# Two streaming encoder layers on one core: sums of squares moved to TensorE, additions to VectorE, eight early products in the first layer

## The chip, the cores and the metric

The kernel runs on one core of one Trainium2 chip. The metric is the device time of one execution in microseconds (us); smaller is better. The five engines of the core run their own queues in order and wait for each other through semaphores. In the profile they are PE (TensorE, with its weight loads as PEld), DVE (VectorE), ACT (ScalarE), POOL (GpSimd) and SP (SyncE, which issues the loads).

## What is computed

A hybrid encoder of two layers works on 256 frames of a new stream and 64 frames of a running one, so 320 token columns with 1024 features. Each layer is a mixer and a ConvFFN, each between two RMS norms. The first layer's mixer is a Mamba-2 scan, the second one's is latent attention (MLA). After the first layer the shared key latent is made from the stream. Cut to what the change touches:

```python
def rmsnorm(x, g):
    y = xf * lax.rsqrt(jnp.mean(xf * xf, axis=-1, keepdims=True) + EPS)
    return y * g
for layer in range(2):
    h = rmsnorm(x, norm_mix_pre[layer])
    mix = mamba2_mixer(h, ...) if layer == 0 else mla_attend(h, ...)
    x = x + rmsnorm(mix, norm_mix_post[layer])
    f = conv_ffn(rmsnorm(x, norm_ffn_pre[layer]), ...)
    x = x + rmsnorm(f, norm_ffn_post[layer])
```

## The kernel before

Features lie on the 128 partitions and tokens on the free axis, so x is eight tiles of 128x320 (k = 0 to 7). Every fp32 product is made of three matmuls of split operands, a high and a low part each (`xgh` and `xgl`, `wh` and `wl`): high by high, low by high, high by low. ACT makes the high parts, DVE the low parts. All weights stream in by SP's loads into `wr` and are split into `wh` and `wl` before use.

**A join** is the place where one part ends and the next begins: `x = x + y * r`, where `y` holds the part's output and `r` the factor of its post norm. There are three joins, and `enter` (boundary=True) writes them: into ffn 0 (at 269 us), into MLA (at 512 us) and into ffn 1 (at 735 us). `late_rstd` sums the squares of the last output on PE, makes the factor on POOL (`newton`), and `spread` broadcasts it over the partitions by three PE transposes into a PSUM tile (`pr` or `px`). Then, for each k, DVE multiplies `y` by the spread tile, adds it to x (POOL does this for k = 3, 5, 7), ACT makes `xgh` and DVE `xgl` one step behind, and ACT squares the new x (`xsq`). POOL adds the squares into `xacc`. The order on DVE and ACT in a join is as written; the other engines' orders come from a scheduler.

The next part's matmuls start with raw x: `outer` runs k over the outside, so that six output blocks (three and three in MLA) take 18 matmuls for each k as soon as `xgh` and `xgl` of that k exist. The factor of the pre norm comes later: `rstd_of` sums `xacc` over the partitions on PE (`toksum`, three 128x1 matmuls), `mean` and `newton` make the factor, and it is spread into `xr` and multiplied onto the block's results. Blocks that come still later use normalized x instead: `normalized` makes `xn` = x times `xr` on POOL and splits it into `xnh` and `xnl`.

**The first layer's start** is `enter` with boundary=False: x is loaded, split and squared, and blocks 0 to 3 are done with k outside. Blocks 3 to 7 of the next loop follow with raw x. The convolutions (`conv`) of the first six blocks are done by a small POOL copy of padding rows into `ext`, two DVE products of the PSUM block with `xr` into `ext` (these free the PSUM buffer), a POOL copy of the saved rows to `ssave`, one ACT and three DVE operations. The eight `xn` steps are put between those blocks, with two `xn` buffers.

Of the kernel before, what the change touches and what calls it, by code (L numbers as in the profile page):

```python
# [11 lines left out]
AF = mybir.ActivationFunctionType  # L12
# [29 lines left out]
RING = 2, 3, 2  # L42
EARLY = 1, 9, 3
HIGH = 2, 0, 2
# [42 lines left out]
class Kern:  # L87
# [254 lines left out]

    def mean(self, src, dim, pool):

        v = self.t(pool, [P, 3], "nwv", bufs=3)
        self.nc.vector.tensor_scalar(v, src, 1.0 / dim, EPS, op0=ALU.mult, op1=ALU.add)
        return v
# [7 lines left out]
    def spread(self, r, ps=None):  # L355

        ps = self.pr() if ps is None else ps
        for c, l0 in enumerate(TOK):
            self.pe_end = self.nc.tensor.transpose(ps[:, l0:l0 + 128], r[:, c:c + 1].to_broadcast([P, P]), self.ident).ins
        return ps[:, :T]  # L360
# [37 lines left out]

    def enter(self, xgp, sp, tag, g=None, boundary=True):

# [5 lines left out]
        xl = self.t(xgp, [P, KD, T], "xgl", F32R, bufs=1)  # L406
        acc = self.t(sp, [P, T], "xacc", bufs=1)
        self.xhigh = []
# [19 lines left out]
        def square(k):  # L428
            if k == 0:
                act(out=acc, in_=self.x[:, k, :], func=AF.Square)  # L430
                return
            s = self.t(sp, [P, T], tag, bufs=2)
            act(out=s, in_=self.x[:, k, :], func=AF.Square)
            nc.gpsimd.tensor_tensor(out=acc, in0=acc, in1=s, op=ALU.add)  # L434

        with self.region if boundary else ExitStack():
            for k in range(KD + 1):
                if k < KD:
                    xk = self.x[:, k, :]
                    if boundary:  # L440
                        yk = self.y[:, k, :]
                        tt(out=yk, in0=yk, in1=r, op=ALU.mult)
                        if k == 0:
                            tt(out=xh[:, k, :], in0=xk, in1=yk, op=ALU.add)
                        e = nc.gpsimd if k in (3, 5, 7) else nc.vector
                        e.tensor_tensor(out=xk, in0=xk, in1=yk, op=ALU.add)
                        if k:
                            high(k)
                        else:
                            low(k)  # L450
                    else:
                        high(k)
                        low(k)
                if boundary and k > 1:
                    low(k - 1)
                if k:
                    square(k - 1)
        if boundary:
            self.ends.pop(0)
        return xh, xl, acc  # L460

    def normalized(self, xgp, sp, g, rstd):

        nc = self.nc
        xh = self.t(xgp, [P, KD, T], "xnh", F32R, bufs=1)
        xl = self.t(xgp, [P, KD, T], "xnl", F32R, bufs=1)

        def step(k):
            xn = self.t(sp, [P, T], "xn", bufs=2)
            nc.gpsimd.tensor_tensor(out=xn, in0=self.x[:, k, :], in1=rstd, op=ALU.mult)  # L470
            self.split(xh[:, k, :], xl[:, k, :], xn, self.v(g, k))

        return xh, xl, [lambda k=k: step(k) for k in range(KD)]
# [115 lines left out]

    def outer(self, nblk, xh, xl, xacc, pool):  # L590
# [51 lines left out]

    def conv(self, ps, rstd, pool, k, pads, w, b, rows_out, dst=None):

# [3 lines left out]
        q = m + TP  # L648
        both = pads.shape[1] == 2 * m
        ext = self.t(pool, [P, 2 * q if both else W], "ext", bufs=3)  # L650
        if both:
            nc.gpsimd.tensor_copy(out=ext.rearrange("p (a b) -> p a b", a=2)[:, :, 0:m], in_=pads.rearrange("p (a b) -> p a b", a=2))
# [8 lines left out]
        if both:  # L661
            nc.gpsimd.tensor_copy(out=rows_out, in_=ext[:, TP:TP + 2 * (TS + m)].rearrange("p (a b) -> p a b", a=2)[:, :, 0:m])
        else:
# [34 lines left out]
    def ssm(self):  # L698
# [3 lines left out]
        with ExitStack() as st:  # L702
# [5 lines left out]
            with ExitStack() as s2:  # L708
# [4 lines left out]
                with ExitStack() as s3:  # L713
# [9 lines left out]
                    self.qd = KD  # L723
                    xh, xl, xacc = self.enter(xtp, dp, "xsq", "mix_pre0", False)
                    ps, rstd = self.outer(4, xh, xl, xacc, dp)
                    self.bt, self.ct, self.xs = {}, {}, {}
                    dt2 = self.ssm_dt(ps[0], rstd, sp, dp)
                    for i in range(1, 4):
                        self.ssm_conv(i - 1, ps[i], rstd, sp)
                    xnh, xnl, steps = self.normalized(xgp, dp, "mix_pre0", rstd)  # L730
                    szs = {0: self.t(sp, [P, 4, T], "sz", bufs=2)}
# [90 lines left out]
    def ssm_conv(self, i, ps, rstd, sp):  # L822
# [7 lines left out]
        else:  # L830
            self.xs[4 * g + i - 2] = dst
        self.conv(ps, rstd, sp, 4, self.v("sst", 6 * blk, 6), lambda j: self.v("scw", 4 * blk + j), self.v("scb", blk),
                  self.ssave[:, blk, :, :], dst)
        self.silu(dst, dst)
# [200 lines left out]
    def ffn(self, i):  # L1035
        nc, a = self.nc, self.a
        with ExitStack() as st:
# [3 lines left out]
            with ExitStack() as s2:  # L1041
                xgp = self.pool(s2, f"xgf{i}")
                sp = self.pool(s2, f"fs{i}")
                fsave = self.t(sp, [P, 44, 2, 2], "fsave")
                xh, xl, xacc = self.enter(xgp, sp, "xsq", f"ffn_pre{i}")
                self.yst.close()
                self.psum(**(PSF, PSL)[i])
                ps, rstd = self.outer(6, xh, xl, xacc, sp)
                self.est.close()
# [41 lines left out]
    def mla(self):  # L1091
        nc, a = self.nc, self.a
        tt, ts, stt = nc.vector.tensor_tensor, nc.vector.tensor_scalar, nc.vector.scalar_tensor_tensor
        with ExitStack() as st:
# [10 lines left out]
            with ExitStack() as s2:  # L1105
# [5 lines left out]
                nc.sync.dma_start(out=oldt, in_=a["oldt"].rearrange("p (a b) -> p a b", a=2))  # L1111
                xh, xl, xacc = self.enter(xgp, sp, "xsq")
                self.yst.close()
# [9 lines left out]
                self.outer_part(kv, range(4, 8), xh, xl)  # L1123
                s = self.t(sp, [P, T], "xsq", bufs=2)
                nc.scalar.activation(out=kacc, in_=kv[0][:, :T], func=AF.Square)
# [36 lines left out]
                for b in range(3):  # L1162
# [395 lines left out]
```

## Time and profile before

| | before |
|---|---|
| time, median of 3 runs | 985.29 us (985.29 to 986.44) |
| profiled execution, its own time | 985.59 us |
| its span | 983.8 us |
| granted PE clock, mean | 0.992 |
| busy DVE, ACT, POOL | 75%, 62%, 36% of the span |

The span is what the profiler sees from the first to the last instruction; the profiled execution's own time is 1.8 us longer than it. In timeline rows the first column is the start in us from the span's start, the second the time from the first start to the last end of the group, then engine, line, operation and its tiles; the brackets at the end give the idle time before it and what ended it. Matmul durations overlap, so the price of one is the distance from start to start. In rows of stretches the pairs are busy time and instructions of PE, PEld, DVE, ACT and POOL, then the granted PE clock (1.00 is full), the DMA share and the rate.

### The profile page before, as it was taken

What the parts mean: (1) busy time and instruction counts of PE and PEld (TensorE: products, weight loads), DVE (VectorE), ACT (ScalarE), POOL (GpSimd) and SP (SyncE); (2) the same over time, 40 slices, a digit from 0 to 9 for tenths busy, and PEclk for the clock granted to TensorE, in tenths of its full rate; (3) what the DMA queues carried; (4) which work ended last, traced back from release to release, by engine and by line L of the source; (5) the groups of instructions that cost most, each with busy time, mean ns of one, the idle gap of its engine ahead of it and who ended that gap; (6) DMA issues with size and microseconds to landing.
All of it is one profiled execution on the core that took longest, in us unless ns stands there. A gap on an engine that the chain in (4) does not pass through costs nothing.

```text
span 983.8 us, 17990 instructions
## 1 busy us (share of the span) xinstructions
PE 960.0 (98%) x6602; PEld 932.7 (95%) x6602; DVE 738.8 (75%) x1348; ACT 614.0 (62%) x1247; POOL 353.5 (36%) x560
## 2 busy tenths in 40 slices
PE   8799999999999999999999999999999999999997
PEld 8799999989989999999999899999999999999996
DVE  7989889975579998765547898885638999775432
ACT  7568988644556787654444677764645678665331
POOL 5822411000056875420017766520005777441000
PEclk9899999999999999999999999999999999999999
DMA  7465646443334545455631222233534454445541
GB/s 256 143 196 181 202 134 204 139 134 118 103 119 131 171 150 172 150 181 165 195 112 37 81 73 76 57 97 108 172 107 127 129 174 151 151 145 147 153 118 54
DMA packets 45945, 135.58 MB, mean 138 GB/s; under 512 B 5408, under 2 KB 10144, under 8 KB 45856
## 3 DMA queue, kind: packets, MB, share of 16 engines
q1 hardware_dynamic: 45712, 134.42, 43.9%
q8 instruction: 52, 0.85, 0.4%
q14 instruction: 37, 0.30, 0.1%
q10 hardware_dynamic: 144, 0.00, 0.0%
HBM read 130.29 MB, written 4.11 MB: 137 GB/s over the span
## 4 chain that ended last, share of the span: by engine, by line
PE 83%; DVE 9%; POOL 3%; ACT 2%; issue 2%; DMA 0%; SPq 0%; POOLq 0%; DVEq 0%; ACTq 0%
PE pm L284 47%; PE pm L285 23%; PE px L284 3%; PE px L285 1%; PE px L987 1%; PE px L970 1%; PE pr L352 1%; POOL xacc L434 1%; DVE wl L329 1%; PE px L978 1%; ACT wh L327 1%; POOL xn L470 1%; DVE xnl L331 1%; DVE cv L670 1%; PE px L953 1%
## 5 line engine op out<-in xcount | busy, mean ns | idle before, releaser
L329 DVE TENSOR_TENSOR wl<-wr,wh 128x1024 fp32r<-128x1024 f32 (+2 forms) x204 | 242.9, 1191 | 108.7 <-ACT wh L327 107.6
L327 ACT ACTIVATE wh<-wr 128x1024 fp32r<-128x1024 f32 (+4 forms) x235 | 227.7, 971 | 149.1 <-PE pm L284 131.5
L284 PE MATMUL pm<-xnh,wh 128*128 128x320 f32 x768 | 239.2, 312 | 0.2 <-DVE ext L660 0.2
L284 PE MATMUL pm<-xnl,wh 128*128 128x320 f32 x768 | 239.3, 312 | 0.0
L285 PE MATMUL pm<-xnh,wl 128*128 128x320 f32 x768 | 238.2, 310 | 0.0
L284 PEld LDWEIGHTS pm<-xnl,wh 128*128 128x128 f32 x768 | 144.2, 188 | 3.0 <-issue 3.0
L285 PEld LDWEIGHTS pm<-xnh,wl 128*128 128x128 f32 x768 | 144.2, 188 | 1.7 <-issue 1.7
L284 PEld LDWEIGHTS pm<-xnh,wh 128*128 128x128 f32 x768 | 144.2, 188 | 1.5 <-issue 0.7
L285 PE MATMUL pm<-ah,wl 128*128 128x320 f32 x424 | 131.3, 310 | 0.0
L284 PE MATMUL pm<-al,wh 128*128 128x320 f32 x424 | 131.2, 310 | 0.0
L284 PE MATMUL pm<-ah,wh 128*128 128x320 f32 x424 | 131.1, 310 | 0.0
L670 DVE SCALAR_TENSOR_TENSOR cv<-ext,vec,cv 128x322 f32<-128x322 f32 x176 | 98.2, 569 | 6.1 <-ACT cv L668 3.6
L664 POOL COPY fsave<-ext 128x2 f32<-128x2 f32 x88 | 71.1, 808 | 50.5 <-ACT ext L658 46.9
L340 POOL TENSOR_TENSOR rk<-nwl,half 128x3 f32<-128x3 f32 x4 | 3.4, 851 | 216.5 <-DVE nwl L391 216.5
L284 PEld LDWEIGHTS pm<-ah,wh 128*128 128x128 f32 x424 | 79.5, 188 | 1.0 <-issue 1.0
L285 PEld LDWEIGHTS pm<-ah,wl 128*128 128x128 f32 x424 | 79.6, 188 | 0.2 <-issue 0.2
L284 PEld LDWEIGHTS pm<-al,wh 128*128 128x128 f32 x424 | 79.6, 188 | 0.0
L284 PE MATMUL pm<-xgh,wh 128*128 128x320 f32 x236 | 68.6, 320 | 7.2 <-ACT xs L689 5.9
L285 PE MATMUL pm<-xgh,wl 128*128 128x320 f32 x236 | 74.2, 317 | 0.7 <-DVE wl L331 0.7
L284 PE MATMUL pm<-xgl,wh 128*128 128x320 f32 x236 | 74.1, 317 | 0.5 <-DVE xgl L418 0.5
L668 ACT ACTIVATE cv<-ext,vec 128x322 f32<-128x322 f32 x88 | 57.0, 653 | 15.1 <-POOL ext L655 9.7
L329 POOL TENSOR_TENSOR wl<-wr,wh 128x512 fp32r<-128x512 f32 (+2 forms) x31 | 43.7, 1424 | 25.2 <-ACT wh L327 22.7
(384 smaller groups left out, 2196.5 us busy)
## 6 DMA issues: line engine op xcount, KB each, us to landing
wr<-w_up SPq DMA_DIRECT2D x76, 512.0 KB, 3.3
wr<-w_in SPq DMA_DIRECT2D x37, 512.0 KB, 3.9
wr<-w_dn SPq DMA_DIRECT2D x32, 512.0 KB, 3.6
wr<-w_out SPq DMA_DIRECT2D x16, 512.0 KB, 3.4
wr<-w_o SPq DMA_DIRECT2D x16, 512.0 KB, 3.3
wr<-w_up_k SPq DMA_DIRECT2D x16, 384.0 KB, 3.4
wr<-w_dn SPq DMA_DIRECT2D x16, 384.0 KB, 3.2
dc<-acd SPq DMA_DIRECT2D x8, 512.0 KB, 6.0
```

Source lines behind the costliest of these rows:

```text
L284: for i in (mm(out, wh, xh, start=first, stop=False), mm(out, wh, xl, start=False, stop=False), mm(out, wl, xh, start=False, stop=last)):
L285: mm(out, wl, xh, start=False, stop=last)):
L327: self.high_ins = nc.scalar.activation(out=hdst, in_=src, func=AF.Copy).ins
L329: return lambda: e.tensor_tensor(out=ldst, in0=src, in1=hdst.bitcast(F32), op=ALU.subtract)
L331: return lambda: nc.vector.scalar_tensor_tensor(out=ldst, in0=src, scalar=scale, in1=hdst.bitcast(F32), op0=ALU.mult, op1=ALU.subtract)
L352: i = self.nc.tensor.matmul(ps[:, o + b:o + b + 1], acc[:, l0:l0 + 128], self.ones[:, 0:1], start=True, stop=True)
L434: nc.gpsimd.tensor_tensor(out=acc, in0=acc, in1=s, op=ALU.add)
L470: nc.gpsimd.tensor_tensor(out=xn, in0=self.x[:, k, :], in1=rstd, op=ALU.mult)
L664: nc.gpsimd.tensor_copy(out=rows_out[:, 0, :], in_=ext[:, TP:TP + m])
L668: nc.scalar.activation(out=c, in_=ext[:, 0:n], func=AF.Identity, scale=w(0), bias=b)
L670: nc.vector.scalar_tensor_tensor(out=c, in0=ext[:, i:i + n], scalar=w(i), in1=c, op0=ALU.mult, op1=ALU.add)
L953: nc.tensor.transpose(xt_[:n, j * 128:j * 128 + 128], xs[j][:, l0:l0 + n], self.ident)
```

## The change

The sums of squares are no longer added up on POOL. `square` now sends each `xsq` straight to PE: three 128x1 matmuls for each k, accumulating in three columns of a PSUM tile. In a join this tile is the spread tile itself, columns 320 to 322, the one that the multiplications of `y` read; in the first layer it is a tile of its own. `mean` reads those columns, and the `toksum` of `xacc` goes. In the joins the additions of x for k = 3, 5, 7 go from POOL to DVE. In the first layer all eight `xn` products are issued at once, ahead of the convolutions, into eight buffers, and the small copies of the first six convolutions go from POOL to ACT. `EARLY` takes one more split weight tile into the first join.

```diff
-EARLY = 1, 9, 3
+EARLY = 2, 9, 3
 def spread(self, r, ps=None):
-        ps = self.pr() if ps is None else ps
+        ps = self.spread_tile = self.pr() if ps is None else ps
 def enter(...):
-        acc = self.t(sp, [P, T], "xacc", bufs=1)
+        sums = self.spread_tile if boundary else self.pr()
...
         def square(k):
-            if k == 0:
-                act(out=acc, in_=self.x[:, k, :], func=AF.Square)
-                return
-            s = self.t(sp, [P, T], tag, bufs=2)
+            s = self.t(sp, [P, T], tag, bufs=3)
             act(out=s, in_=self.x[:, k, :], func=AF.Square)
-            nc.gpsimd.tensor_tensor(out=acc, in0=acc, in1=s, op=ALU.add)
+            for b, l0 in enumerate(TOK):
+                nc.tensor.matmul(sums[:, T + b:T + b + 1], s[:, l0:l0 + 128], self.ones[:, 0:1], start=k == b == 0, stop=k == KD - 1 and b == 2)
...
-                        e = nc.gpsimd if k in (3, 5, 7) else nc.vector
-                        e.tensor_tensor(out=xk, in0=xk, in1=yk, op=ALU.add)
+                        tt(out=xk, in0=xk, in1=yk, op=ALU.add)
...
-        return xh, xl, acc
+        return xh, xl, self.mean(sums[:, T:T + 3], D, sp, mean)
 def normalized(..., ahead=False):
+        def product(k):
+            xn = self.t(sp, [P, T], "xn", bufs=KD if ahead else 2)
+            nc.gpsimd.tensor_tensor(out=xn, in0=self.x[:, k, :], in1=rstd, op=ALU.mult)
+            return xn
+        done = [product(k) for k in range(KD)] if ahead else []
         def step(k):
-            xn = self.t(sp, [P, T], "xn", bufs=2)
-            nc.gpsimd.tensor_tensor(out=xn, in0=self.x[:, k, :], in1=rstd, op=ALU.mult)
-            self.split(xh[:, k, :], xl[:, k, :], xn, self.v(g, k))
+            self.split(xh[:, k, :], xl[:, k, :], done[k] if ahead else product(k), self.v(g, k))
 def outer(...):
-        r = self.rstd_of(xacc, D, pool)
+        r = self.newton(xv, pool, "rk")
 def conv(..., act=False):
+        def copy(o, i):
+            if act:
+                nc.scalar.activation(out=o, in_=i, func=AF.Copy)
+            else:
+                nc.gpsimd.tensor_copy(out=o, in_=i)
...
```

The places where the order moves are these. First PE at the join into ffn 1, from the end of the matmuls on `warm` that fill the wait for the factor. Before:

```order
L365 LDWEIGHTS warm_75
L365 MATMUL pm_9082<-warm_75 128x256
L583 MATMUL pm_9191<-xgh_9122,wh_8963 128x320
L583 MATMUL pm_9192<-xgh_9122,wh_8963 128x320
L583 MATMUL pm_9193<-xgh_9122,wh_8963 128x320
L583 MATMUL pm_9194<-xgh_9122,wh_8963 128x320
```

Now:

```order
L365 LDWEIGHTS warm_75
L365 MATMUL pm_9123<-warm_75 128x256
L432 MATMUL px_9141<-ones_73,xsq_9172 128x1 x3
L432 MATMUL px_9141<-ones_73,xsq_9182 128x1 x3
L432 MATMUL px_9141<-ones_73,xsq_9192 128x1 x3
L432 MATMUL px_9141<-ones_73,xsq_9201 128x1 x3
L432 MATMUL px_9141<-ones_73,xsq_9210 128x1 x3
L432 MATMUL px_9141<-ones_73,xsq_9219 128x1 x3
L432 MATMUL px_9141<-ones_73,xsq_9228 128x1 x3
L432 MATMUL px_9141<-ones_73,xsq_9234 128x1 x3
L585 MATMUL pm_9251<-xgh_9163,wh_9004 128x320
```

All eight sums (one `xsq` for each k) stand ahead of the first product of `xgh`. Second, PE at the join into ffn 0, at the products of k = 1; the join into MLA has the same pattern. Before:

```order
L284 MATMUL pm_3275<-xgh_3201,wh_3071 128x320
L284 MATMUL pm_3276<-xgh_3201,wh_3071 128x320
L284 MATMUL pm_3271<-xgl_3202,wh_3071 128x320
L285 MATMUL pm_3271<-xgh_3201,wl_3072 128x320
L284 MATMUL pm_3272<-xgl_3202,wh_3071 128x320
```

Now:

```order
L284 MATMUL pm_3314<-xgh_3221,wh_3091 128x320
L284 MATMUL pm_3315<-xgh_3221,wh_3091 128x320
L432 MATMUL pr_3199<-ones_73,xsq_3230 128x1 x3
L284 MATMUL pm_3310<-xgl_3222,wh_3091 128x320
L285 MATMUL pm_3310<-xgh_3221,wl_3092 128x320
L284 MATMUL pm_3311<-xgl_3222,wh_3091 128x320
```

The sum of k = 0 stands between the six products of `xgh` and the twelve that follow; the sum of k = 1 stands at the same place of k = 2, and so on. Third, DVE in the same join, with what each row waits for (a name such as PE_49 is the semaphore of that engine). Before, k = 2 and 3:

```order
L442 TENSOR_TENSOR y_2529<-y_2529,pr_3179 128x320
L446 TENSOR_TENSOR x_72<-x_72,y_2529 128x320 [waits DVE_49]
L418 SCALAR_TENSOR_TENSOR xgl_3202<-x_72,vec_70,xgh_3201 128x320 [waits Activation_49]
L329 TENSOR_TENSOR wl_3194<-wr_3033,wh_3193 128x768 [waits DMAHW6_49]
L442 TENSOR_TENSOR y_2529<-y_2529,pr_3179 128x320
```

Now:

```order
L440 TENSOR_TENSOR y_2543<-y_2543,pr_3199 128x320 [waits PE_49]
L443 TENSOR_TENSOR x_72<-x_72,y_2543 128x320 [waits DVE_49]
L418 SCALAR_TENSOR_TENSOR xgl_3222<-x_72,vec_70,xgh_3221 128x320 [waits Activation_49]
L329 TENSOR_TENSOR wl_3214<-wr_3053,wh_3213 128x768 [waits DMAHW7_49]
L440 TENSOR_TENSOR y_2543<-y_2543,pr_3199 128x320 [waits PE_49]
L443 TENSOR_TENSOR x_72<-x_72,y_2543 128x320 [waits DVE_49]
```

The multiplication of `y` for k of 2 and more waits for PE now: in the program its count is that of the sum of k - 2, which writes the tile that it reads. The `xgl` between them is that of k - 1.

More of the change, by code (lines that the diff above doesn't have):

```diff
@@ L341, in newton, with mean @@
         return r
-    def mean(self, src, dim, pool):
-        v = self.t(pool, [P, 3], "nwv", bufs=3)
+    def mean(self, src, dim, pool, v=None):
+        v = self.t(pool, [P, 3], "nwv", bufs=3) if v is None else v
         self.nc.vector.tensor_scalar(v, src, 1.0 / dim, EPS, op0=ALU.mult, op1=ALU.add)
@@ L397, in late_rstd, with enter @@
         return ps
-    def enter(self, xgp, sp, tag, g=None, boundary=True):
+    def enter(self, xgp, sp, tag, g=None, boundary=True, mean=None):
         nc = self.nc
@@ L459, in enter, with normalized @@
             self.ends.pop(0)
-        return xh, xl, acc
-    def normalized(self, xgp, sp, g, rstd):
+        return xh, xl, self.mean(sums[:, T:T + 3], D, sp, mean)
+    def normalized(self, xgp, sp, g, rstd, ahead=False):
         nc = self.nc
@@ L588, in outer_part, with outer @@
             self.mm3(ps[b][:, :T], w[k][0][:, s], w[k][1][:, s], xh[:, k, :], xl[:, k, :], k == 0, k == KD - 1, behind)
-    def outer(self, nblk, xh, xl, xacc, pool):
+    def outer(self, nblk, xh, xl, xv, pool):
         ps = [self.pm() for _ in range(nblk)]
@@ L641, in run, with conv @@
         self.pst.close()
-    def conv(self, ps, rstd, pool, k, pads, w, b, rows_out, dst=None):
+    def conv(self, ps, rstd, pool, k, pads, w, b, rows_out, dst=None, act=False):
         nc = self.nc
@@ L649, in conv @@
         both = pads.shape[1] == 2 * m
+        def copy(o, i):
[3 more added lines that the diff above has]
+                nc.gpsimd.tensor_copy(out=o, in_=i)
         ext = self.t(pool, [P, 2 * q if both else W], "ext", bufs=3)
         if both:
-            nc.gpsimd.tensor_copy(out=ext.rearrange("p (a b) -> p a b", a=2)[:, :, 0:m], in_=pads.rearrange("p (a b) -> p a b", a=2))
+            copy(ext.rearrange("p (a b) -> p a b", a=2)[:, :, 0:m], pads.rearrange("p (a b) -> p a b", a=2))
         else:
@@ L661, in conv @@
         if both:
-            nc.gpsimd.tensor_copy(out=rows_out, in_=ext[:, TP:TP + 2 * (TS + m)].rearrange("p (a b) -> p a b", a=2)[:, :, 0:m])
+            copy(rows_out, ext[:, TP:TP + 2 * (TS + m)].rearrange("p (a b) -> p a b", a=2)[:, :, 0:m])
         else:
@@ L723, in ssm @@
                     self.qd = KD
-                    xh, xl, xacc = self.enter(xtp, dp, "xsq", "mix_pre0", False)
-                    ps, rstd = self.outer(4, xh, xl, xacc, dp)
+                    xh, xl, xv = self.enter(xtp, dp, "xsq", "mix_pre0", False)
+                    ps, rstd = self.outer(4, xh, xl, xv, dp)
                     self.bt, self.ct, self.xs = {}, {}, {}
                     dt2 = self.ssm_dt(ps[0], rstd, sp, dp)
+                    xnh, xnl, steps = self.normalized(xgp, dp, "mix_pre0", rstd, True)
                     for i in range(1, 4):
                         self.ssm_conv(i - 1, ps[i], rstd, sp)
-                    xnh, xnl, steps = self.normalized(xgp, dp, "mix_pre0", rstd)
                     szs = {0: self.t(sp, [P, 4, T], "sz", bufs=2)}
@@ L832, in ssm_conv @@
         self.conv(ps, rstd, sp, 4, self.v("sst", 6 * blk, 6), lambda j: self.v("scw", 4 * blk + j), self.v("scb", blk),
-                  self.ssave[:, blk, :, :], dst)
+                  self.ssave[:, blk, :, :], dst, g == 0)
         self.silu(dst, dst)
@@ L1044, in ffn @@
                 fsave = self.t(sp, [P, 44, 2, 2], "fsave")
-                xh, xl, xacc = self.enter(xgp, sp, "xsq", f"ffn_pre{i}")
+                xh, xl, xv = self.enter(xgp, sp, "xsq", f"ffn_pre{i}")
                 self.yst.close()
                 self.psum(**(PSF, PSL)[i])
-                ps, rstd = self.outer(6, xh, xl, xacc, sp)
+                ps, rstd = self.outer(6, xh, xl, xv, sp)
                 self.est.close()
@@ L1111, in mla @@
                 nc.sync.dma_start(out=oldt, in_=a["oldt"].rearrange("p (a b) -> p a b", a=2))
-                xh, xl, xacc = self.enter(xgp, sp, "xsq")
+                vs = self.t(sp, [P, 6], "vs")
+                xh, xl, _ = self.enter(xgp, sp, "xsq", mean=vs[:, 0:3])
                 self.yst.close()
@@ L1123, in mla @@
                 self.outer_part(kv, range(4, 8), xh, xl)
-                s = self.t(sp, [P, T], "xsq", bufs=2)
+                s = self.t(sp, [P, T], "xsq", bufs=3)
                 nc.scalar.activation(out=kacc, in_=kv[0][:, :T], func=AF.Square)
@@ L1136, in mla @@
                 pt = self.pr()
-                self.toksum(xacc, pt)
                 self.toksum(kacc, pt, 3)
-                vs = self.t(sp, [P, 6], "vs")
                 ex = self.t(sp, [P, 3], "ex")
-                ts(vs[:, 0:3], pt[:, 0:3], 1.0 / D, EPS, op0=ALU.mult, op1=ALU.add)
                 ts(ex, vs[:, 0:3], EPS, None, op0=ALU.mult)
@@ L1167, in mla @@
                     else:
-                        s = self.t(sp, [P, T], "xsq", bufs=2)
+                        s = self.t(sp, [P, T], "xsq", bufs=3)
                         nc.scalar.activation(out=s, in_=ps[b][:, :T], func=AF.Square)
```

## The prediction

> **What bounds the kernel now.** I read the busy shares first, then PE's waits, then the joins in the timeline. The first line of the page says that PE is the bound:
>
> ```profile
> PE 960.0 (98%) x6602; PEld 932.7 (95%) x6602; DVE 738.8 (75%) x1348; ACT 614.0 (62%) x1247; POOL 353.5 (36%) x560
> ```
>
> With 24 us of idle PE in the span, a change gains only by taking away a PE wait or PE work. PE's waits by releaser, the four that the change can touch (total, times, longest):
>
> ```profile
> PE pm L284 <- ACT xs L689: 5.9, 1, 5.9
> PE pm L284 <- ACT wh L330: 1.3, 1, 1.3
> PE pr L352 <- POOL xacc L434: 0.9, 1, 0.9
> PE pm L285 <- DVE wl L331: 0.7, 1, 0.7
> ```
>
> The first is the one large stall, in the first layer. The timeline around it:
>
> ```profile
> 33.81 0.55 DVE L331 SCALAR_TENSOR_TENSOR xnl<-xn,vec,xnh 128x320 fp32r<-128x320 f32 x1 [1.51 <-ACT xnh L330]
> 34.44 1.13 POOL L470 TENSOR_TENSOR xn<-x,xr 128x320 f32<-128x320 f32 x1 [0.43 <-DVE xnl L331]
> 34.75 1.17 DVE L331 SCALAR_TENSOR_TENSOR xnl<-xn,vec,xnh 128x320 fp32r<-128x320 f32 x1
> 35.03 0.31 PE L284 MATMUL pm<-xgh,wh 128*128 128x320 f32 x1
> 35.18 0.31 PE L284 MATMUL pm<-xgl,wh 128*128 128x320 f32 x1
> ...
> 43.07 0.54 DVE L660 TENSOR_TENSOR ext<-pm,xr 128x256 f32<-128x256 f32 x2
> 43.75 0.60 PE L284 MATMUL pm<-xgh,wh 128*128 128x320 f32 x1 [5.92 <-ACT xs L689]
> 44.16 0.47 PE L284 MATMUL pm<-xgl,wh 128*128 128x320 f32 x1
> 44.42 0.47 PE L285 MATMUL pm<-xgh,wl 128*128 128x320 f32 x1
> ```
>
> The wait is put down to a SiLU on ACT, but what it really needs is a PSUM buffer: block 7 takes that of block 3, and DVE's `ext` at 43.07 frees it. A matmul costs 0.15 us here (35.03 to 35.18) and 0.26 us after the stall (44.16 to 44.42), so the clock is halved too:
>
> ```profile
> 45.00:50.00 5.00, 5.00 (x22) 5.00 (x22) 5.00 (x13) 1.46 (x4) 3.41 (x2) 0.56 0.33 108
> ```
>
> A clock of 0.56 over 5 us loses 5 x 0.44 = 2.2 us. The stall is worth 5.9 + 2.2 = 8.1 us, about as much as all else that the change could gain.
>
> **The joins.** The join into ffn 0, with DVE's steps and PE's answers:
>
> ```profile
> 268.68 0.49 DVE L442 TENSOR_TENSOR y<-y,pr 128x320 f32<-128x320 f32 x1 [1.72 <-PE pr L359]
> 269.20 0.49 DVE L444 TENSOR_TENSOR xgh<-x,y 128x320 fp32r<-128x320 f32 x1
> 269.72 0.49 DVE L446 TENSOR_TENSOR x<-x,y 128x320 f32<-128x320 f32 x1
> 269.74 1.14 PE L583 MATMUL pm<-xgh,wh 128*128 128x320 f32 x6
> 270.66 0.48 DVE L442 TENSOR_TENSOR y<-y,pr 128x320 f32<-128x320 f32 x1
> 271.18 0.49 DVE L446 TENSOR_TENSOR x<-x,y 128x320 f32<-128x320 f32 x1
> 271.59 0.48 DVE L442 TENSOR_TENSOR y<-y,pr 128x320 f32<-128x320 f32 x1
> 272.48 1.04 PE L284 MATMUL pm<-xgh,wh 128*128 128x320 f32 x6
> 272.51 0.55 DVE L418 SCALAR_TENSOR_TENSOR xgl<-x,vec,xgh 128x320 fp32r<-128x320 f32 x1
> 272.98 0.95 DVE L329 TENSOR_TENSOR wl<-wr,wh 128x768 fp32r<-128x768 f32 x1
> 273.10 0.46 ACT L433 ACTIVATE xsq<-x 128x320 f32<-128x320 f32 x1
> 273.84 0.48 DVE L442 TENSOR_TENSOR y<-y,pr 128x320 f32<-128x320 f32 x1
> ```
>
> From start to start `y` takes 0.52 us, the addition to x 0.41, `xgl` 0.47 and `wl` 0.86. PE takes the 18 matmuls of a k in 2.7 us (269.74 to 272.48) and never waits for the join's chain: DVE runs ahead of PE, 1.4 us for a k.
>
> **What the change does in the joins into ffn 0 and MLA.** The new sums write the tile that `y` reads. The program turns this into waits in both directions: a sum of k waits until DVE's `y` of k + 1 has read the tile, and `y` of k + 2 waits for the sum of k. DVE can no longer run ahead. PE's order for each k is six products of `xgh` (A), the sum of k - 1 (S), twelve products with `xgl` (B). B needs `xgl` of k, and that stands in DVE's queue behind `y` and the addition of k + 1, which may begin only after S. So PE idles after each S while DVE does 0.52 + 0.41 + 0.55 = 1.48 us, and 0.05 us for each of two crossings (`xgh` ends at 269.20 + 0.49 = 269.69, and PE starts on it at 269.74): 1.6 us, for k = 1 to 6. That is 6 x 1.6 = **9.6 us in each of the two joins**. Queued behind the waiting `y` stand `xgl` and the `wl` of coming weights; ACT's `xgh` of the next k waits for the addition and is there by the end of B.
>
> The price of a sum comes from the toksum of the second layer's entry:
>
> ```profile
> 505.25 0.72 PE L352 MATMUL pr<-ones,yacc 128*128 128x1 f32 x6
> 505.84 0.39 PE L284 MATMUL pm<-ah,wh 128*128 128x320 f32 x1
> ```
>
> Three 128x1 matmuls take 0.59 us of PE. Eight sums in place of one toksum cost 7 x 0.59 = 4.1 us in each join (nothing at the least, if PE does them while it would wait; these stand ahead of the wait, so I take the row). Against this the waits of 1.3 and 0.7 us in ffn 0 go, since DVE and ACT get 10 us more for the weights: -2.0.
>
> The clock. Stretches of 4 us with idle time, and those after them:
>
> ```profile
> 16.00:20.00 4.00, 3.12 (x23) 2.85 (x22) 3.75 (x9) 2.49 (x4) 2.84 (x5) 1.00 0.45 182
> 20.00:24.00 4.00, 3.88 (x28) 3.62 (x27) 3.33 (x7) 1.98 (x4) 2.85 (x3) 1.00 0.52 147
> ...
> 284.00:288.00 4.00, 2.46 (x16) 1.94 (x14) 3.42 (x4) 2.83 (x6) 3.20 (x3) 1.00 0.38 131
> 288.00:292.00 4.00, 3.59 (x13) 3.35 (x14) 1.36 (x3) 1.45 (x3) 1.63 (x1) 0.57 0.61 171
> 540.00:544.00 4.00, 3.10 (x22) 2.73 (x21) 3.85 (x6) 2.00 (x5) 4.00 (x4) 1.00 0.16 26
> 544.00:548.00 4.00, 3.59 (x15) 3.44 (x14) 3.02 (x10) 2.94 (x8) 3.79 (x5) 0.57 0.59 187
> ...
> 648.00:652.00 4.00, 3.06 (x23) 2.71 (x21) 3.54 (x13) 2.41 (x9) 0.62 (x2) 1.00 0.40 131
> 652.00:656.00 4.00, 3.80 (x30) 3.64 (x30) 3.98 (x14) 3.33 (x11) 0.00 (x0) 1.00 0.01 4
> ```
>
> Of four stretches with 2.5 to 3.1 us of busy PE two were followed by a clock of 0.57, which loses 4 x 0.43 = 1.7 us; two were not. With 1.6 us idle in every 4.8 us PE is busy for 2.7 us of 4, between these rows and nearer the 2.46. A join lasts about 30 us, so up to seven stretches; a halved clock fills the gaps and lets it recover, so I take two dips, 3.4 us, for each of the two joins, with none and four as bounds. In ffn 0 the dip at 288, whose cause goes, comes off: -1.7.
>
> [...]
>
> **The join into ffn 1.** Here all eight sums stand ahead of the first product, so PE waits for the whole chain: y0 to y3 as in the rows, 273.84 - 268.68 = 5.16 us with one `wl`; then y3, x3, `xgl`, `wl` 2.26; three times `y`, x, `xgl` 4.2; y7 and x7 1.0: 12.6. `xsq` 0.46, the sum 0.59 and crossings of 0.1 make 13.8 us after y0. Before:
>
> ```profile
> 734.95 0.49 DVE L442 TENSOR_TENSOR y<-y,px 128x320 f32<-128x320 f32 x1 [1.72 <-PE px L359]
> 736.01 1.14 PE L583 MATMUL pm<-xgh,wh 128*128 128x320 f32 x6
> ```
>
> PE started 1.1 us after y0, so it loses **12.7 us**. The clock after it is halved as after the stall of 5.9 us: 2.2. The later toksum goes: -0.6. Together +14.3 (to +16 if `y` also waits for the sums by 0.2 us a step).
>
> **The first layer.** The eight sums (4.1 us by the row above, less the toksum's wait of 0.9) come while PE waits for loads and splits; the stretch 16 to 20 shows 0.9 us idle. I take 0 for them, and +3 as the bound. The stall: `ext` of block 3 stands behind about as many DVE rows as before, one `xnl` more (0.55), but the 1.51 us in which DVE waited for POOL's `xn` at 33.81 goes. So it comes about 1 us earlier: -1. Its bounds are wide, since DVE's two-input operations double beside POOL's (`xnl` 0.55 at 33.81, 1.17 at 34.75 beside `xn`) and eight products in a row now meet other rows: five such more or fewer are 3 us either way, and if block 7 never waits all 8.1 go. The small copies on ACT have slack in the stall: 0 (POOL's copies take 0.5 or less on their own).
>
> [...]
>
> **The sum**, on the profiled execution's 985.6 us (0.3 above the median):
> - ffn 0: 9.6 + 4.1 - 2.0 + 3.4 - 1.7 = +13.4
> - MLA: 9.6 + 4.1 + 3.4 = +17.1
> - ffn 1: 12.7 + 2.2 - 0.6 = +14.3
> - first layer: -1
>
> Together +43.8: **1029.4 us**. Everything else runs by PE with no wait, and only its order moves: 0.
>
> **The rivals.**
> - [...] Chance 0.2.
> - Gates hold and the clock dips in four stretches in each of the two joins: +6.8, 1036; with the sums' bound in the first layer and late sums in ffn 1, 1041. Chance 0.15.
> - The gates don't bind in ffn 0 and MLA (DVE's waits end before they are reached), only ffn 1 stalls: 985.6 + 14.3 + 2 x 4.1 - 3.7 - 1 = 1003.4. Against it: PE meets S before B in its queue, so S cannot be early. Chance 0.08.
> - Faster: the stall at 37.8 to 43.8 goes, and none of the joins waits. The place is DVE's `ext` of block 3: once it comes before 37.8, 8.1 us go, 2.0 and 1.7 in ffn 0 and the 0.9 of the first toksum. The sums in the joins must then cost less than these 12.7: at half the row's price, 12.3 / 2 = 6.2, the time is 979. It decides where DVE is not held at all; the waits in the program speak against it. Chance 0.04.
> - The change does nothing that can be seen, gains and sums cancelling (the case before at the row's full price: 985): 0.03.
>
> **How the numbers follow.** My forecast has 0.5. The range is to hold eight in ten: it leaves out the last two cases, half of the one in which only ffn 1 stalls, and the ends of that with four dips: 1003 to 1042. A difference under 0.2%, 2 us, can't be told from none. Faster 0.05, same 0.03, slower 0.92.
>
> **What would show it.** Right: in the joins into ffn 0 and MLA PE waits for `xgl`, about 1.6 us, six times each; in ffn 1 one wait of 12 us or more ahead of L585, released through `xsq`; DVE idle ahead of `y`, released by PE's L432. Wrong: `y` that starts before the sum of two steps earlier, PE going on through S to B without a gap, or a first stall gone that outweighs the joins.

## The result and the profile after

The changed kernel takes 1067.86 us (median of 6 runs, 1059.6 to 1077.7) against 985.29 us: a ratio of 1.0835, 95% interval 1.0802 to 1.0868. It is slower, as forecast, but by 83 us where 44 were forecast, and above the range. Ratios here leave out runs more than 1.5% above the fastest of the same kernel. The profiled execution took 1064.75 us with a span of 1063.0.

The first line of the page and PE's four largest waits:

```profile
PE 1007.6 (95%) x6770; PEld 980.2 (92%) x6770; DVE 730.1 (69%) x1357; ACT 615.2 (58%) x1259; POOL 306.9 (29%) x511
...
PE px L432 <- ACT xsq L430: 15.3, 7, 2.9
PE pm L284 <- DVE xgl L418: 9.4, 6, 1.6
PE pm L284 <- DVE xgl L421: 9.0, 6, 1.5
PE pm L284 <- DVE ext L669: 5.5, 2, 5.3
```

PE is busy for 47.6 us more than before and idle for 31.6 us more. The idle part is the first three rows: the six gaps of 1.6 us in each of ffn 0 and MLA, and the wait of ffn 1. The busy part is mostly not more work: the change adds the work of 28 sums of 0.59 us, 16.5 us (eight in place of one toksum, in three joins and the first layer). The rest is the same work at a lower clock (mean granted clock 0.955, before 0.992).

The spread of the factor (L359) marks each join's beginning, and the next one its end, so the execution can be cut there. In ffn 0 after the change (start, length, engine, line, tiles):

```profile
270.51 0.49 PE L359 MATMUL pr<-con,rk 128*128 128x128 f32 x3
321.55 0.49 PE L359 MATMUL pr<-con,rk 128*128 128x128 f32 x3
```

From the same rows of both kernels:

| stretch, us | before | after | difference | forecast |
|---|---|---|---|---|
| start to the spread of ffn 0 | 268.15 | 270.51 | +2.4 | -1 |
| join into ffn 0 | 28.51 | 51.04 | +22.5 | +13.4 |
| to the spread of MLA | 214.81 | 214.80 | 0 | 0 |
| join into MLA | 23.56 | 50.92 | +27.4 | +17.1 |
| to the spread of ffn 1 | 199.39 | 199.44 | 0 | 0 |
| join into ffn 1 | 22.97 | 48.53 | +25.6 | +14.3 |
| rest | 226.4 | 227.8 | +1.4 | 0 |

The loss lies where the forecast has it, and each join loses about 10 us more. The 1.4 us of the last row belong to the join into ffn 1: before, 135 of its products stand ahead of the spread that ends it, after the change 126, and the other nine (0.147 us each, 1.3 us) come behind that mark. In the other two joins the number is the same in both kernels (150 and 135). In ffn 0 the first gap looks as predicted (the sum, the wait, and DVE's chain that PE waits for):

```profile
275.73 0.72 PE L432 MATMUL pr<-ones,xsq 128*128 128x1 f32 x6
278.02 0.41 PE L284 MATMUL pm<-xgl,wh 128*128 128x320 f32 x1 [1.57 <-DVE xgl L418]
...
276.49 0.49 DVE L440 TENSOR_TENSOR y<-y,pr 128x320 f32<-128x320 f32 x1 [2.46 <-PE pr L432]
277.01 0.49 DVE L443 TENSOR_TENSOR x<-x,y 128x320 f32<-128x320 f32 x1
277.42 0.54 DVE L418 SCALAR_TENSOR_TENSOR xgl<-x,vec,xgh 128x320 fp32r<-128x320 f32 x1
```

DVE had been idle for 2.46 us, until the sum ended; `y`, the addition and `xgl` follow, and PE starts 1.57 us after it stopped. What was not predicted is the clock (the column after POOL's pair):

```profile
276.00:280.00 4.00, 2.43 (x18) 2.35 (x18) 2.31 (x4) 0.93 (x2) 0.00 (x0) 1.00 0.07 8
284.00:288.00 4.00, 4.00 (x20) 3.97 (x19) 0.00 (x0) 0.00 (x0) 0.00 (x0) 0.60 0.43 131
308.00:312.00 4.00, 2.62 (x10) 2.62 (x11) 2.90 (x6) 3.10 (x7) 0.00 (x0) 0.50 0.00 0
316.00:320.00 4.00, 4.00 (x17) 4.00 (x16) 2.03 (x3) 0.69 (x1) 0.47 (x1) 0.50 0.68 211
320.00:324.00 4.00, 4.00 (x26) 3.99 (x25) 1.47 (x3) 1.57 (x3) 0.75 (x1) 0.83 0.32 116
```

From 284 to 320 it is never full for long: each time PE works through (284 to 288, 20 matmuls in 4 us where 27 would fit) it does so at a clock of 0.50 to 0.60. In the trace's record of this run the granted clock changes at distances of 3.41 us or whole multiples of it, and so it does in the kernel before. Cut at its changes, the same stretch is:

```profile
283.80:287.22 3.42, 3.42 (x15) 3.42 (x14) 0.07 (x1) 0.00 (x0) 0.00 (x0) 0.50 0.50 153
287.22:290.63 3.41, 1.84 (x15) 1.76 (x14) 1.44 (x3) 0.92 (x2) 0.00 (x0) 1.00 0.00 0
290.63:294.04 3.41, 3.41 (x15) 3.41 (x15) 0.00 (x0) 0.00 (x0) 0.00 (x0) 0.50 0.00 0
294.04:297.46 3.42, 1.85 (x13) 1.77 (x14) 1.49 (x4) 1.66 (x3) 0.00 (x0) 1.00 0.02 5
297.46:300.87 3.41, 3.41 (x17) 3.41 (x15) 0.91 (x1) 0.00 (x0) 0.00 (x0) 0.50 0.40 138
300.87:304.28 3.41, 1.84 (x13) 1.75 (x14) 1.44 (x3) 0.92 (x2) 0.00 (x0) 1.00 0.04 16
304.28:321.35 17.07, 15.50 (x63) 15.42 (x62) 6.91 (x12) 5.52 (x10) 0.90 (x1) 0.50 0.39 118
```

Each of the three full steps here, with a gap in it (1.84 or 1.85 us of busy PE, 0.35 to 0.72 us of it in a sum), is followed by a halved one. Eight steps are halved in ffn 0 (the last row holds five), and nine in MLA.

In ffn 1, PE, DVE and ACT over one step of the join:

```profile
794.12 1.44 PE L432 MATMUL px<-ones,xsq 128*128 128x1 f32 x6 [2.06 <-ACT xsq L430]
797.62 1.44 PE L432 MATMUL px<-ones,xsq 128*128 128x1 f32 x6 [2.06 <-ACT xsq L430]
...
814.20 1.95 PE L585 MATMUL pm<-xgh,wh 128*128 128x320 f32 x6
...
795.60 0.49 DVE L440 TENSOR_TENSOR y<-y,px 128x320 f32<-128x320 f32 x1 [1.16 <-PE px L432]
796.12 0.49 DVE L443 TENSOR_TENSOR x<-x,y 128x320 f32<-128x320 f32 x1
...
796.64 0.56 ACT L411 ACTIVATE xgh<-x,vec 128x320 fp32r<-128x320 f32 x1 [2.58 <-DVE x L443]
797.11 0.45 ACT L430 ACTIVATE xsq<-x 128x320 f32<-128x320 f32 x1
```

This is a ring. A sum ends at 795.56, `y` starts at 795.60, the addition follows, ACT makes `xgh` from it, and only then the square that belongs to the k before; then comes the next sum. One turn takes 3.5 us for a k, and no two steps overlap. The first product starts 27.5 us after the spread, where it was 1.6.

### The profile page after: what moved, and what is told of

Its sections match the earlier page's. It is cut to its first block, busy times and chain, and to the rows that moved or that the text cites. A ratio compares the mean times of both kernels' runs of the same rounds, so it can differ in the third digit from the quotient of the medians.

```text
span 1063.0 us, 18301 instructions
## 1 busy us (share of the span) xinstructions
PE 1007.6 (95%) x6770; PEld 980.2 (92%) x6770; DVE 730.1 (69%) x1357; ACT 615.2 (58%) x1259; POOL 306.9 (29%) x511
## 4 chain that ended last, share of the span: by engine, by line
PE 84%; DVE 9%; issue 2%; ACT 1%; POOL 1%; DVEq 0%; ACTq 0%; POOLq 0%
PE pm L284 46%; PE pm L285 23%; PE px L284 3%; PE px L285 1%; PE pr L432 1%; PE px L996 1%; PE px L432 1%; PE pm L585 1%; PE px L979 1%; DVE y L440 1%; POOL xn L467 1%; DVE x L443 1%; PE px L987 1%; PE pr L352 1%; DVE cv L679 1%
## 5 line engine op out<-in xcount | busy, mean ns | idle before, releaser
L329 DVE TENSOR_TENSOR wl<-wr,wh 128x1024 fp32r<-128x1024 f32 (+3 forms) x203 | 239.0, 1179 | 121.6 <-ACT wh L327 121.0
L327 ACT ACTIVATE wh<-wr 128x1024 fp32r<-128x1024 f32 (+4 forms) x234 | 226.4, 972 | 162.5 <-PE pm L284 132.6
L673 POOL COPY fsave<-ext 128x2 f32<-128x2 f32 x88 | 74.6, 847 | 44.8 <-ACT ext L667 40.0
L284 PE MATMUL pm<-xgh,wh 128*128 128x320 f32 x230 | 71.2, 337 | 6.4 <-DVE ext L669 5.3
```

Of the source, the lines that this page charges most:

```text
L284: for i in (mm(out, wh, xh, start=first, stop=False), mm(out, wh, xl, start=False, stop=False), mm(out, wl, xh, start=False, stop=last)):
L327: self.high_ins = nc.scalar.activation(out=hdst, in_=src, func=AF.Copy).ins
L329: return lambda: e.tensor_tensor(out=ldst, in0=src, in1=hdst.bitcast(F32), op=ALU.subtract)
L673: nc.gpsimd.tensor_copy(out=rows_out[:, 0, :], in_=ext[:, TP:TP + m])
```

## The experiments

Thirteen kernels ran, each beside the kernel before, which had a median of 983.9 to 985.0 us. A kernel that ran once has one time and no ratio.

**A copy of the factor, so that no `y` waits for a sum.**

```diff
         sums = self.spread_tile if boundary else self.pr()
+        if boundary:
+            rs = self.t(sp, [P, T], "rs", bufs=1)
+            act(out=rs, in_=r, func=AF.Copy)
+            r = rs
```

> y is multiplied by a copy of the spread factor in SBUF (one ACT copy more per join, two xsq buffers), so no y waits for a sum; the sums stay where they are. If the shared tile makes the gaps: the six PE waits for xgl in ffn 0 and in MLA go, the clock stays near 1.0 there, spread to spread falls from 51.0 to about 31 us in ffn 0 (28.5 before, plus 4.1 for the sums, 0.5 for the copy, less 2.0) and from 50.9 to about 28 in MLA; ffn 1 still waits for all sums ahead of its first product, but without the ring: about 38 instead of 48.5. In all about 1011 us. If the place of the sums between the products makes the gaps, whatever tile they write: they stay, and the time stays over 1045.

One run: 1013.42 us, clock 0.988. Spread to spread 26.5, 30.2 and 38.4 us (in ffn 0, 24 of the 150 products, 3.5 us, come behind the mark here). PE's largest waits:

```profile
PE pm L284 <- DVE ext L673: 5.3, 1, 5.3
PE px L436 <- ACT xsq L434: 5.2, 3, 3.9
PE pm L589 <- DVE xgh L446: 3.1, 2, 2.1
```

The waits for `xgl` are gone, with the sums still among the products. So the shared tile makes the gaps, not the place of the sums. In ffn 1 the first product comes 17.7 us after the spread instead of 27.5; what is left there is the order, all sums ahead of it.

**Squares ahead of `xgh` on ACT.** In a join, the square of k - 1 is issued just ahead of `high(k)`; its sum stays where the code had it.

```diff
                         if k:
+                            s = square(k - 1)
                             high(k)
...
                 if k:
-                    square(k - 1)
+                    add_up(k - 1, s if boundary and k < KD else square(k - 1))
```

> ACT squares x of k - 1 ahead of the xgh of k instead of behind it; nothing else. If the join into ffn 1 is a ring in which each sum waits for the xgh of the next k on ACT, its step falls from 3.5 us to about 1.5 to 2.2, the first product comes about 10 us earlier, and the whole is about 1053 us; ffn 0 and MLA keep their gaps of 1.6 us. If the ring runs through DVE and PE alone: no change, 1065.

One run: 1027.37 us, clock 0.984. Spread to spread 29.2, 32.4 and 38.3 us; this execution also began slowly (first spread at 36.0 us where the changed kernel had 22.7, see below), so the joins show more than the total. ffn 1 went as the ring has it. ffn 0 and MLA were a miss: their gaps were expected to stay and went. With the squares ready sooner, the scheduler put each sum one k earlier; after the six products of k = 2 now stands the sum of that k:

```
L284 MATMUL pm_3315<-xgh_3221,eh_487_3009 128x320
L435 MATMUL pr_3199<-ones_73,xsq_3247 128x1 x3
L284 MATMUL pm_3310<-xgl_3222,eh_487_3009 128x320
```

`xsq_3247` is the square of k = 2 (that of k = 1 stood here). DVE is released one step earlier, which is all it needed: `y` is still gated, but PE is no longer late. The price of the gate is set by how far ahead of its use the releasing instruction stands.

**The change without the sums in the joins**: POOL adds the squares there as before; additions on DVE, the early tile and the first layer as changed.

```diff
+            if not boundary:
+                s = self.t(sp, [P, T], tag, bufs=3)
+                act(out=s, in_=self.x[:, k, :], func=AF.Square)
+                for b, l0 in enumerate(TOK):
+                    nc.tensor.matmul(sums[:, b:b + 1], s[:, l0:l0 + 128], self.ones[:, 0:1], ...)
+                return
             if k == 0:
                 act(out=acc, in_=self.x[:, k, :], func=AF.Square)
```

> The change without the sums on PE in the joins: there POOL adds the squares up as before, and one toksum follows; the additions on DVE, the longer early list and the whole first layer are as changed. If the sums make all of the loss in the joins: the joins last as before (28.5, 23.6 and 23.0 us spread to spread, each within 1), and the whole is 985.3 plus the 2.4 us that the first layer lost, 985 to 989. If the additions on DVE or the early tile take part: joins over 26 and 31, over 995.

984.13 us against 984.99, ratio 1.0008 (0.9986 to 1.003). Spread to spread 24.1, 23.8 and 23.0 us. So the sums in the joins are the whole of their loss, and the rest of the change gains in ffn 0, where no change had been forecast. The 4.4 us are not all gain: nine of the 150 products come behind the mark here. From the spread of ffn 0 to that of MLA the run is 3.7 us shorter than before. PE's waits for weights are down from 2.0 to 0.5 us, and there is no dip of the clock (mean granted clock 0.995 over the run, before 0.992).

**Matmuls in the gaps.** Matmuls on the `warm` tile, 128x256, into a PSUM tile that nobody reads, behind each sum:

```diff
+    def dummy(self, ps, n, e):
+        for _ in range(n):
+            i = self.nc.tensor.matmul(ps[:, 256:], self.warm[:, 0:128], self.warm[:, 0:256], start=True, stop=True).ins
+            self.after(i, e)
+            e = i
```

> The change with 13 matmuls on the warm tile behind each sum in ffn 0 and MLA and 16 in ffn 1, in the time in which PE waits; the gates stay. If the rest of the loss is the clock, and the clock is lost through the gaps: it stays near 1.0 in all three joins, spread to spread is 28.5 + 9.4 + 4.1 - 2.0 = 40 in ffn 0, 23.6 + 9.0 + 4.1 = 37 in MLA and about 44 in ffn 1 (the ring at 2.9 us a step), the whole about 1035 us. If the clock has nothing to do with the gaps, or the added matmuls delay the products: 1065 or more.

> As the run with matmuls in the gaps, but with 5 instead of 13 in ffn 0 and MLA and 6 instead of 16 in ffn 1, so about 1.0 us of each gap of 1.6 stays idle. If the clock goes by gaps of that order however short: ffn 0 near 51 and MLA near 51, over 1055. If shorter gaps keep it: 40 and 41, the whole about 1040 to 1045, with ffn 1 nearer to the changed kernel's 48.5 since about 1.4 us of each wait stay.

1045.54 us with 13 (clock 0.992) and 1047.98 with 5 (0.980), one run each. Spread to spread 39.4, 41.2 and 44.5 us with 13; 39.4, 41.2 and 48.9 with 5. Stretches in ffn 0, of 13 and then of 5:

```profile
283.00:287.00 4.00, 3.95 (x30) 3.89 (x31) 1.31 (x2) 0.49 (x2) 0.00 (x0) 1.00 0.29 98
```

```profile
283.00:287.00 4.00, 3.00 (x22) 2.91 (x21) 1.88 (x4) 0.92 (x2) 0.00 (x0) 1.00 0.23 59
287.00:291.00 4.00, 3.00 (x23) 2.68 (x24) 1.44 (x3) 0.92 (x2) 0.00 (x0) 1.00 0.18 72
```

The gates are as they were, and the joins into ffn 0 and MLA, with as many products as in the changed kernel, are 11.6 and 9.7 us shorter: that is what the clock cost there, at the least. It is full except for one step of 3.41 us in MLA (568.69 to 572.10 with 13), behind a wait of 1.6 us for `vs` that the filler doesn't reach. The whole is 10 us over the expected 1035, since this run's start was 5 us later than the changed kernel's and MLA 4 us longer than worked out. Five short matmuls in a gap, which leave PE idle for 1.0 us in 4, do as much as thirteen. In ffn 1 six are too few: the wait is longer there, and the join is as long as without.

**The first layer alone, and its parts.** The kernel before with the change's first layer; with its products and ACT copies alone; with its sums alone.

```diff
-                    for i in range(1, 4):
-                        self.ssm_conv(i - 1, ps[i], rstd, sp)
-                    xnh, xnl, steps = self.normalized(xgp, dp, "mix_pre0", rstd)
+                    xnh, xnl, steps = self.normalized(xgp, dp, "mix_pre0", rstd, True)
+                    for i in range(1, 4):
+                        self.ssm_conv(i - 1, ps[i], rstd, sp)
```

> The kernel before with the first layer of the change alone: sums on PE, eight early products, copies on ACT; the joins are as before. The first spread comes at 22.6 us and the stall ahead of block 7 stays at 5.3 us, so the first layer gains or loses about 1 us: 984 to 988. If the start of the first layer takes part in the changed kernel's scatter (1059.6 to 1077.7), the times of this kernel reach over several us more than those of before, with the time up to the first spread going along. If the scatter is of the joins alone, they lie as close as before.

> The first layer's early products and copies on ACT alone; the squares are added on POOL as before. If the sums on PE cost the first layer its 11 us: TensorE is at full rate from about 8 us on as before (25 matmuls or more in each 4 us), the times lie as close as before's, 983 to 987. If the products or the copies cost it: about 996, with scatter.

> The first layer's sums on PE alone; products and copies as before. If the sums keep the clock low at the start: 18 matmuls in 4 us for some of the time from 4 to 32 us, first spread anywhere from 22 to 36 us, times scattered over 986 to 1000. If they don't: 984 to 986, close together.

| | time, us | ratio to before |
|---|---|---|
| first layer | 996.36 (986.71 to 1000.01) | 1.0101 (1.0054 to 1.0148) |
| products and copies | 984.84 (982.9 to 986.98) | 1.0009 (0.9998 to 1.002) |
| sums | 1001.48 (990.77 to 1003.48) | 1.0166 (1.0126 to 1.0205) |

The forecast for the first (984 to 988) was a miss, that for the products a hit. The stall ahead of block 7 is 5.3 us with the whole first layer, 5.9 before: the early products bring nothing else. With the sums the time differs from run to run: 2 to 15 us over before with the whole first layer, 7 to 19 with the sums alone. The reason is in the start of the first layer's profiled run, beside the one with products alone:

```profile
12.00:16.00 4.00, 4.00 (x18) 4.00 (x18) 1.46 (x3) 1.54 (x3) 0.00 (x0) 1.00 1.01 378
24.00:28.00 4.00, 4.00 (x19) 4.00 (x19) 0.00 (x0) 0.63 (x1) 0.00 (x0) 1.00 0.00 0
32.00:36.00 4.00, 4.00 (x25) 3.99 (x24) 2.14 (x4) 1.91 (x4) 0.00 (x0) 1.00 0.33 88
```

```profile
8.00:12.00 4.00, 4.00 (x27) 4.00 (x27) 3.82 (x5) 4.00 (x10) 3.14 (x3) 1.00 1.04 379
```

PE was never idle from 8 to 32 us, yet it did 16 to 19 matmuls in 4 us instead of 27, and its first spread came at 35.8 us instead of 21.4. (The clock column reads 1.00 there since the trace's record of the clock begins with its first change, here to full at 33.5 us; the matmuls' distances are what counts.) The sums stand in between, the last at 26.8; at 33.4, 5.3 us after it had ended, the distance falls from 0.27 to 0.15 us.

Seven of the profiled kernels have this same first layer, and they differ. Their clock is first full at 3.9, 4.9, 10.1, 10.2, 15.7, 33.5 and 33.9 us, and the first spread follows at 22.7, 22.7, 25.0, 25.1, 27.6, 35.8 and 36.0. In the first two, the changed kernel and the run without sums in the joins, the clock was full before the first sum (5.5 us) and stayed so. So in these two runs the sums did not halve a clock that was full; in the other five, where it was not full yet when they began, it rose only at 10.1 to 33.9 us. The ten times of the run without sums in the joins (982.8 to 989.4) show that 1.0101 is the ratio of these six runs, not a fixed price. In the profiled run of the sums alone the clock was full from 10.3 us and the first spread came at 25.1, but 4 us more were lost from there to the spread at 243.4 us (235.5 before); why is not known.

**The joins of the change with the first layer of before.**

> The joins of the change with the first layer of before. If the changed kernel's loss is the joins' plus the first layer's: spread to spread 51, 51 and 48.5 us as there, the whole 985 + 79 less 1.2 = about 1061 to 1063, and the scatter (1059.6 to 1077.7) is down to some 4 us. If the scatter is of the joins: it stays near 15 us.

1061.08 us (1056.61 to 1064.77, 4 runs), ratio 1.0784 (1.0753 to 1.0815); spread to spread 52.2, 51.0 and 48.4 us. The scatter is 8 us instead of 18: more than expected, so part of it is the joins' own. That the upper part comes from the first layer fits, with four runs against six, but isn't shown.

**The sums in one group** behind the products of k = 5 instead of one by one between the products:

```diff
+            for k, s in enumerate(late):
+                for c, l0 in enumerate(TOK):
+                    i = self.nc.tensor.matmul(sums[:, c:c + 1], s[:, l0:l0 + 128], self.ones[:, 0:1], ...).ins
+                    if k == c == 0:
+                        self.after(i, self.last_prod)
```

> As the run with the first layer's sums on PE alone, but all eight sums in one group behind the products of k = 5 (eight square buffers instead of three); as many matmuls, another place. If it is their place between the products that keeps the clock low at the start: full rate from about 8 us on (25 matmuls or more in each 4 us from 8 to 20 us), first spread at 21 to 24 us, 983 to 987 us, close together. If the sums themselves or their number do it: first spread up to 36 us and a scatter over 990 to 1003 as there.

990.93 us (988.66 to 994.44), ratio 1.0065 (1.0045 to 1.0085). The start is at full rate from about 9 us (26 matmuls from 8 to 12 us, 29 from 12 to 16) and the scatter is 6 us instead of 13, as the place would have it; but the first spread is at 26.0, because of what the group itself does (L617 is the group):

```profile
17.26 0.31 PE L285 MATMUL pm<-xgh,wl 128*128 128x320 f32 x1
17.41 5.41 PE L617 MATMUL pr<-ones,xsq 128*128 128x1 f32 x48
22.68 0.59 PE L284 MATMUL pm<-xgh,wh 128*128 128x320 f32 x1
23.07 0.47 PE L284 MATMUL pm<-xgl,wh 128*128 128x320 f32 x1
23.34 0.47 PE L285 MATMUL pm<-xgh,wl 128*128 128x320 f32 x1
```

```profile
16.00:20.00 4.00, 4.00 (x35) 4.00 (x34) 1.58 (x4) 2.48 (x4) 0.38 (x3) 1.00 0.56 225
20.00:24.00 4.00, 4.00 (x31) 4.00 (x31) 1.14 (x3) 0.00 (x0) 0.90 (x1) 0.84 0.43 131
24.00:28.00 4.00, 4.00 (x23) 3.96 (x22) 1.40 (x3) 1.56 (x3) 0.39 (x2) 0.73 0.40 131
```

At the end of 5.4 us of nothing but 128x1 matmuls, PE busy throughout, the clock fell (0.84 and 0.73 in the rows above), and the products behind them start 0.27 us apart. So neither reading was whole: the place matters for the start, and a block of the sums by itself was followed by a halved clock.

**What the good parts are worth.** The kernel before with the early tile alone, with the additions alone, with both.

```diff
-EARLY = 1, 9, 3
+EARLY = 2, 9, 3
...
-                        e = nc.gpsimd if k in (3, 5, 7) else nc.vector
+                        e = nc.vector
```

> The kernel before with the longer early list alone (2 instead of 1 in the first join). If the 4.4 us that the run without sums gained in the join into ffn 0 come from the second early tile, this has them: spread to spread 24 instead of 28.5 us, no waits for wh and wl there, 980 to 982. If they come from the additions on DVE: 985.

> The kernel before with the three additions of each join on DVE alone. If they make the gain in the join into ffn 0: 24 us there and 980 to 982. If the early tile makes it: no difference that can be measured, 985, with the joins within 1 us of before (DVE has 1.2 us more in each join and no contention with POOL).

> The kernel before with the additions on DVE and the longer early list, nothing else. Each alone took 3.2 us off by taking the waits and the dip from the join into ffn 0; they take away the same waits, so together little more: 24.1 us spread to spread there, 980 to 981.5. If they add up: 978 to 979.

| | time, us | ratio to before | join into ffn 0 |
|---|---|---|---|
| early tile | 981.78 (980.23 to 984.25) | 0.9977 (0.9963 to 0.9991) | 24.2 |
| additions | 981.81 (981.34 to 985.25) | 0.9979 (0.9965 to 0.9993) | 25.1 |
| both | 980.66 (979.84 to 982.79) | 0.9970 (0.9957 to 0.9983) | 24.4 |

The forecasts of a winner between the first two were a miss: each has a gain, and both together hardly more. The column overstates it, since 9 to 13 products come behind the mark in these joins: counted on to the spread of MLA, the three runs are 3.0, 2.7 and 3.4 us shorter than before. About 1 us of that is the dip, and the dip doesn't come in every run: the run with the whole first layer and the one with products and copies have the join as before, with the same waits, and no dip (27.5 us instead of 28.5). The additions alone keep the wait for `wh` (1.5 us) and had no dip behind it (clock 1.00 from 284 to 292 us). The last kernel has the lowest median of this study, below both kernels compared, but its interval overlaps those of the two parts.

## Why the prediction was wrong

**The gates in ffn 0 and MLA: right.** "6 x 1.6 = 9.6 us in each" was 9.4 and 9.0, and the copy of the factor showed the cause. With the clock held full, ffn 0 takes 39.4 us; the terms without the clock, 9.6 + 4.1 - 2.0 - 1.7 on 28.5, give 38.5. In MLA they give 37.3 where 41.2 was measured; of those 4 us, 1.6 are the PE wait for `vs` and about 1.5 the halved step behind it (13 products 0.26 us apart).

**The clock: the step that failed first.** "A halved clock fills the gaps and lets it recover, so I take two dips, 3.4 us": with four as the bound, 6.8. The runs with filler show 11.6 and 9.7 us. The price of a dip was right: a halved step of 3.41 us loses 1.7 us of work. The number was wrong: eight such steps in ffn 0 and nine in MLA, where two were taken and four were the bound. The halved clock didn't fill the gaps: PE still waits 1.6 us after each sum, and the sum itself grows to 1.27 us in ffn 0, so that wait and sum are 2.2 to 2.8 us in each period of the join. The clock did come back three times in ffn 0, at 287.22, 294.04 and 300.87, but the next gap fell into each of those steps, and a halved step followed: a gap of 1.6 us with a sum of 0.6 us was enough, and from 283.80 to 304.28 the clock went to and fro with every step. From 304.28 on it came back only at 321.35, 6.2 us after the products behind the last sum had begun. I priced by rows in which one gap stood alone, and they don't tell how many dips follow where gap follows gap.

**ffn 1: a chain read too short.** "PE waits for the whole chain: 12.6", with steps of 1.4 us for a k on DVE alone, and 0.2 us a step more as the bound. The sum of k needs the square of k, and ACT makes that only after `xgh` of k + 1, as the code has it in `enter`: `high(k)` stands ahead of `square(k - 1)`. So each turn goes through DVE, ACT and PE, 0.52 + 0.52 + 0.47 + 0.46 + 0.83 and crossings: 2.9 us with the clock held (the run with filler has its sums 2.89 us apart), 3.5 with it halved. I had the waits in both directions and did not close them into a ring. The squares-first run shows it: the first product came 18.1 us after the spread instead of 27.5. The other term of this join, 2.2 us for a halved clock behind the wait, was about right: the 126 products take 21.0 us up to the next spread, where 0.147 us each would be 18.5.

**The first layer: right where it was small, wrong about the sums.** The stall was forecast to come about 1 us earlier and was 0.6 us shorter, 5.3 instead of 5.9. "I take 0 for them, and +3 as the bound" is the term that failed: with the sums alone the time was 1.66% longer, and in the run with the whole first layer the start was at half rate up to 33.4 us (0.27 us from matmul to matmul, 0.15 behind it). In the changed kernel's profiled execution the clock was full from 3.9 us on, so its own 79 us hold little of this; its other runs, up to 1077.7, may.

**The rest was as forecast**: the stretches between the joins did not move (0.0 and 0.1 us), and the waits of 2.0 us for weights in ffn 0 went with the additions on DVE and the early tile. That the dip at 288 went with them isn't shown, since two runs without them had no dip there.

## What to carry to other kernels

- Before a result is put into spare columns of a tile that another engine is reading, ask whether waits are kept for each tile: here 24 tiny matmuls put DVE, ACT and PE into lockstep, though no byte is shared. A private copy of the read data removed it, and so did an order in which the release comes one step earlier.
- Close every pair of opposite waits into a ring and add up one turn, with every instruction that an in-order engine puts ahead of the one that releases. The turn, not the slowest engine, is the price of a step.
- The short gaps that recurred here cost twice: in ffn 0 9.4 us as waits and, by the run with filler, 11.6 us at the least by the clock. Price the clock over the whole stretch, step by step (eight and nine halved steps here), not as a fixed number of dips.

## What the runs showed of the hardware that was not expected

- With 128x1 matmuls alone the clock did not stay up here, though the profile shows PE as busy: in the run with the sums in one group a block of 48 rows of them (5.4 us) was followed by a halved clock (products 0.27 us apart), and in the run with the first layer alone, with the sums between the products, PE did 16 to 19 matmuls in each 4 us from 8 to 32 us.
- How the clock followed the work is seen step by step in the changed kernel's join into ffn 0. The three full steps from 287.22, 294.04 and 300.87 had 1.84 or 1.85 us of busy PE each, and a halved one followed each of them. The halved steps from 283.80, 290.63 and 297.46 were busy throughout (3.41 us, of it 0.00, 0.26 and 0.72 in sums), and a full one followed each of them. Of the five halved steps from 304.28 on, the second had 1.85 us of busy PE and the others 3.41; the sums had 1.15, 0.12, 1.77, 0.78 and 0.00 us of it, and only the last one was followed by a full one. How much work holds a clock or brings it back isn't shown by that.
- The same gaps did not always cost a dip. The two waits (2.0 us) in the join into ffn 0 had a halved step of 3.41 us behind them before, and none in the run with products and copies. In the stretches below they lie almost wholly in one row before, and in two rows in that run; that this made the difference is an estimate from these two runs (first the kernel before, whose second row is halved, then that run, with no dip):

```profile
284.92:288.33 3.41, 1.54 (x9) 1.02 (x7) 2.83 (x5) 3.16 (x7) 2.28 (x3) 1.00 0.45 154
288.33:291.74 3.41, 3.33 (x12) 3.09 (x13) 1.03 (x2) 1.11 (x2) 1.63 (x1) 0.50 0.68 186
```

```profile
285.09:288.50 3.41, 2.14 (x14) 1.73 (x12) 2.84 (x4) 2.44 (x5) 3.01 (x3) 1.00 0.46 154
288.50:291.91 3.41, 2.42 (x15) 2.04 (x15) 1.76 (x3) 1.84 (x4) 1.64 (x1) 1.00 0.54 161
```

- Five 128x256 matmuls (0.70 to 0.71 us from the first start to the last end) in each gap of 1.6 us, which left 1.0 us of it idle, were followed by no dip in ffn 0: the clock was 1.00 in every stretch of 4 us from 271 to 311 us, with 3.00 us of busy PE in several of them, where the same join without them had eight halved steps.
